# The own term of the second mixer as a row sum: one change to an encoder trunk kernel on one Trainium2 core

## The chip, the cores and the metric

The kernel runs on one core of a Trainium2 chip. The core has five engines that run side by side, each through its own list of instructions in order: TensorE (PE, matrix products into the PSUM memory; its weight loads are listed apart as PEld), VectorE (DVE), ScalarE (ACT), GpSimd (POOL, which cannot read PSUM) and SyncE (SP, which here only issues DMAs). They wait for each other through semaphores. The metric is the device time of one execution in microseconds, median over runs.

## The reference

A trunk of two layers over 256 tokens of width 2048, float32. Each layer adds a token mixer and a gated feed-forward block with a depthwise convolution, each behind an RMSNorm; a last RMSNorm closes it. The first mixer is a bidirectional mLSTM with 8 heads. The second one, which the change touches, is a bidirectional gated linear recurrence (HGRN2) with 16 heads of 128 keys and 128 values. For one direction of a head:

```python
def _hgrn_chunk(s_st, xs):
    q, k, lf, v = xs
    L = q.shape[2]
    b = jnp.cumsum(lf, axis=2)
    lower = jnp.tril(jnp.ones((L, L), dtype=bool))
    rel = jnp.where(lower[:, :, None], b[:, :, :, None, :] - b[:, :, None, :, :], -jnp.inf)
    attn = jnp.einsum('bhtsk,bhsk->bhts', jnp.exp(rel) * q[:, :, :, None, :], k)
    o = jnp.einsum('bhts,bhsv->bhtv', attn, v) + jnp.einsum('bhtk,bhkv->bhtv', q * jnp.exp(b), s_st)
...
    y = hgrn_direction(q, k_f, lf_f, v) + fl(hgrn_direction(fl(q), fl(k_b), fl(lf_b), fl(v)))
    y = y.reshape(b, s, B_V).astype(hn.dtype)
    y = head_rmsnorm(y, head_g, B_HEADS) * jax.nn.silu(g)
    return y @ w_out
```

A token is in the sum of both directions, and for s = t the decay is exp(0) = 1. So token t contributes to its own output v[t] times the sum over the keys of q[t] * (k_f[t] + k_b[t]). This is the own term.

## The kernel before

**Projections.** Tokens lie along the free axis and features on the 128 partitions. The weights stream from HBM in pieces (`split_weights`): a DMA brings 128x2048 float32, ScalarE rounds a half of it to `wh` (L145) and VectorE forms the rest `wl` (L146). `stream` then walks a list of chunks. A "fm" chunk gives two blocks of 128 features over 256 tokens; for each of its 16 slices of the depth PE does a product of 512 columns (L196) and one of 256 (L197) per block. A "tm" chunk gives 512 features with tokens on the partitions, three products of 512 columns (L186 to L188) per slice and token half. When a chunk is done its function `done` takes the result out of PSUM.

**Side work.** The work of a mixer's heads is written as Python generators that yield a delay. `Side.tick` is called between the products of the stream and resumes each generator whose delay has passed. So the small products of a head stand between the large ones of the projections in PE's list. The program is then put in order by a scheduler that works with its own estimate of times, and this order is fixed in the built program: on the chip each engine takes its list as it stands, and PE cannot go past a small product whose operands are late.

**A head of the second mixer.** Four heads form a quad; per quad there are six fm chunks (q and the two gates of each head), a tm chunk for V after the third and one for the output gate at the end. `take` turns a chunk's block into z, the gates g (ScalarE's sigmoid, VectorE's L586), the keys `KZ` of both directions, and on GpSimd the products q*g (`QZ`, L587), a copy of g (L589) and `ks`, the sum of the two keys (L592). With the second gate the generator `head` is pushed.

`head` builds the 256x256 matrix `AT` of weights between tokens. It starts with the own term: PE multiplies ks by q for each half of the tokens (L616; the whole 128x128 block, of which only the diagonal is wanted), and VectorE's `put` copies it into AT under the mask `ident` (L604, a copy under a predicate). Then a step passes (`yield step`, 2.4 in the scheduler's units, 1.9 for the last two heads). Then come seven levels of blocks of 1, 2, 4, ... 64 tokens. In each level PE multiplies the gathered keys `km` by the gathered queries `qm` (L626), VectorE multiplies KZ and QZ by the gates of that level (L627, L628) and gathers for the next level (L609), GpSimd multiplies the gates pairwise (L633), and `put` copies the level's part into AT under its mask. Last come the two blocks off the diagonal (L638 to L640), the product of AT with V into `py` (L651), a copy of it to `y` by ScalarE (L652) and the sums of squares (L655). `finish` normalises y and multiplies it by the gate (L666), transposes it (L672) and stores it for the output projection.

**GpSimd and VectorE beside each other.** Per head GpSimd does about ten instructions, nearly all of them in one burst when the second gate is there. The norm of each layer (L253) holds another product with a column of ones: the squares as the stationary operand, `ones[:, 0:1]` as the moving one.

Of the kernel before, what the change touches and what calls it, by code (L numbers as in the profile page):

```python
# [8 lines left out]
F32 = mybir.dt.float32  # L9
# [3 lines left out]
ALU = mybir.AluOpType  # L13
PSUM = bass.MemoryType.PSUM

P = 128
T = 256
# [35 lines left out]
def trunk_kernel(ctx, tc, xT, pp_d, cst_d, w_first, w_aq, w_ak, w_av, w_ao, w_aout,  # L53
                 w_bq, w_bv, w_bg, w_bout, w_up, w_down, out, mscr, stop=9):
    nc = tc.nc
    act, dve, pool, pe = nc.scalar, nc.vector, nc.gpsimd, nc.tensor
# [9 lines left out]
    ones = keep.tile([P, T], F32, name="ones")  # L66
# [4 lines left out]
    ident = cst[:, C_ID:C_ID + P]  # L71
# [5 lines left out]
    def aux(name):  # L77
        return psa.tile([P, 512], F32, tag="aux", name=name)
# [132 lines left out]
    def fm_scaled(ps, R, dst, scale=None):  # L211
        fm_sum(ps, dst)
        if scale is None:
            dve.tensor_tensor(dst, dst, R, ALU.mult)
        else:
            dve.scalar_tensor_tensor(dst, dst, scale, R, ALU.mult, ALU.mult)
# [75 lines left out]
    def head_scale(ss, width):  # L292
        rs = ev.tile([P, 2], F32, tag="rs", bufs=6, name="rs")
        dve.tensor_scalar(rs, ss, 1.0 / width, EPS, ALU.mult, ALU.add)
        pool.tensor_tensor(rs, rs, hmx, ALU.pow)
        return rs
# [238 lines left out]
    def hgrn(norm, nxt):  # L535
# [24 lines left out]
        def blocks(z, h, a, b):  # L560
            v = z[:, 0:2 * (T + h)].rearrange("k (p x) -> k p x", p=2)[:, :, a:b]
            return v.rearrange("k p (m j) -> k m p j", j=2 * h)[:, :, :, 0:h]

        def gview(g, n, start, h):
            v = g[:, start:start + 2 * (n - 1)].rearrange("k (p x) -> k p x", p=2)[:, :, 0::2]
            return v.rearrange("k p m -> k m p").unsqueeze(3).broadcast_to([P, n // 2, 2, h])

        def take(hd, what, ps):
            mp = box["mp"]
            st = heads[hd]  # L570
            if what == 0:
                st["q"] = mp.tile([P, T], F32, tag="q", bufs=2, name="q")
                fm_scaled(ps, norm.R, st["q"], box["oml"][:, hd:hd + 1])
                st["QK"] = mp.tile([P, 1152], F32, tag="QK", bufs=2, name="QK")
                st["G"] = mp.tile([P, 768], F32, tag="G0", bufs=2, name="G")
                return
            dr = what - 1
            lb, oml = box["lb"], box["oml"]
            QZ, KZ, G = st["QK"][:, 0:512], st["QK"][:, 512:1024], st["G"]
            z = mp.tile([P, T], F32, tag="z", bufs=2, name="z")  # L580
            fm_scaled(ps, norm.R, z)
            g = G[:, dr * T:(dr + 1) * T]
            kz = KZ[:, dr * T:(dr + 1) * T]
            act.activation(g, z, AF.Sigmoid)
            act.activation(kz, z, AF.Sigmoid, scale=-1.0)
            dve.tensor_scalar(g, g, oml[:, hd:hd + 1], lb[:, hd:hd + 1], ALU.mult, ALU.add)  # L586
            pool.tensor_tensor(QZ[:, (1 - dr) * T:(2 - dr) * T], st["q"], g, ALU.mult)  # L587
            if dr == 0:
                pool.tensor_copy(G[:, 512:768], g)  # L589
            else:  # L590
                st["ks"] = mp.tile([P, T], F32, tag="ks", bufs=2, name="ks")
                pool.tensor_tensor(st["ks"], KZ[:, 0:T], KZ[:, T:2 * T], ALU.add)  # L592
                side.push(head(hd))

        def head(hd):
            mp = box["mp"]
            st = heads[hd]
            QZ, KZ = st["QK"][:, 0:640], st["QK"][:, 512:1152]
            q, ks, G = st["q"], st["ks"], st["G"]
            AT = mp.tile([P, 4, P], F32, tag="AT", bufs=2, name="AT")  # L600
            pool.memset(AT[:, 0::3], 0.0)

            def put(ps, mask):
                dve.copy_predicated(AT[:, 0::3], mask.bitcast(I32).unsqueeze(1).broadcast_to([P, 2, P]),  # L604
                                    ps[:, 0:T].rearrange("p (a b) -> p a b", a=2))

            def gather(z, h, tag):
                m = mp.tile([P, T], F32, tag=tag, bufs=MIX, name=tag)
                dve.tensor_copy(m.rearrange("k (m p j) -> k m p j", p=2, j=h), blocks(z, h, 0, T))  # L609
                return m  # L610

            km, qm = gather(KZ, 1, "km"), gather(QZ, 1, "qm")
            pd = aux("pd")
            for t in range(2):
                c = slice(t * P, (t + 1) * P)
                pe.matmul(pd[:, c], ks[:, c], q[:, c], start=True, stop=True)  # L616
            put(pd, ident)
            step = SPREAD if hd < BH - 2 else STEP
            yield step
            n = T  # L620
            for li, h in enumerate(LEVELS):
                pd = aux("pd")
                qa, ka = blocks(QZ, h, 0, T), blocks(KZ, h, 0, T)
                for t in range(2):
                    c = slice(t * P, (t + 1) * P)
                    pe.matmul(pd[:, c], km[:, c], qm[:, c], start=True, stop=True)  # L626
                dve.tensor_tensor(ka, ka, gview(G, n, 1, h), ALU.mult)  # L627
                dve.tensor_tensor(qa, qa, gview(G, n, n + 1, h), ALU.mult)  # L628
                if h < 64:
                    km, qm = gather(KZ, 2 * h, "km"), gather(QZ, 2 * h, "qm")  # L630
                    n //= 2
                    G2 = mp.tile([P, 3 * n], F32, tag=f"G{h}", bufs=2, name="G2")
                    pool.tensor_tensor(G2, G[:, 0:6 * n:2], G[:, 1:6 * n:2], ALU.mult)  # L633
                    G = G2
                put(pd, cst[:, C_LV + li * P:C_LV + (li + 1) * P])
                yield step
            pd = aux("pd")
            pe.matmul(pd[:, 0:P], KZ[:, 0:P], QZ[:, T + P:2 * T], start=True, stop=True)  # L638
            pe.matmul(pd[:, P:T], KZ[:, T + P:2 * T], QZ[:, 0:P], start=True, stop=True)
            act.copy(AT[:, 1:3], pd[:, 0:T].rearrange("p (a b) -> p a b", a=2))  # L640
            yield
            while "V" not in st["qd"]:
                yield
            V, j = st["qd"]["V"], hd % 4
            py = aux("py")
            y = mp.tile([P, T], F32, tag="y", bufs=4, name="y")
            ss = mp.tile([P, 2], F32, tag="ss", bufs=2, name="ss")
            for t in range(2):
                c = slice(t * P, (t + 1) * P)
                for s in range(2):  # L650
                    pe.matmul(py[:, c], AT[:, 2 * s + t], V[:, s, j * P:(j + 1) * P], start=(s == 0), stop=(s == 1))  # L651
            act.copy(y, py[:, 0:T])  # L652
            for t in range(2):
                jk = ev.tile([P, T], F32, tag="jk", bufs=1, name="jk")
                act.activation(jk[:, 0:P], y[:, t * P:(t + 1) * P], AF.Square, accum_out=ss[:, t:t + 1])  # L655
            st["y"] = (y, head_scale(ss, 128))
# [109 lines left out]
    if stop > 1:  # L766
        c, close0 = ffn(0, n1, n2)
        chunks += c
    if stop > 2:
        c = hgrn(n2, n3)  # L770
# [7 lines left out]
    if stop > 3:  # L778
        c, close1 = ffn(1, n3, nf)
# [93 lines left out]
```

## Time and profile before

| | |
|---|---|
| median of 3 runs | 2469.77 us (2469.3 to 2469.8) |
| the profiled execution: its time | 2469.78 us |
| the profiled execution: its span | 2468.0 us |
| mean clock granted to PE | 0.998 |
| second mixer's heads | about 1146 to 1650 us of the span |

The profile is one execution recorded by the hardware. Its page lists the busy time of each engine, a picture of the span in slices, the chain of work that ended last (followed back from the last instruction to whatever released it), and the costliest groups of instructions with line, engine, operation, operands and shapes, count, busy time, mean duration in ns, and the idle time of the engine ahead of them with what ended it. Further views of the same trace give busy times in stretches of the span, and single instructions in order of time. There a row shows start and duration in us, engine, line and operands; instructions of the same group that follow each other share a row. A float32 product appears as two records. Durations of products overlap on PE, so the step from one start to the next is the price of a product in the stream, not its duration. The line of a helper (such as L604 in `put`) gathers all uses of the helper.

### The profile page before, as it was taken

Reading aid. Unit: us, or ns where it says so; the run is one execution under the profiler, and the core shown is the slowest. Engines: PE = TensorE matmul, PEld = TensorE weight load, DVE = VectorE, ACT = ScalarE, POOL = GpSimd, SP = SyncE. Lnnn points to the kernel's source line nnn. Section 1 sums busy time; section 2 is a strip of 40 time slices with the busy share of each in tenths; the row PEclk is TensorE's granted clock in tenths of the full one; section 3 lists DMA queues with packets and bytes.
Section 4 is the critical chain, followed back from the end, with each engine's and each line's share of the span. In section 5 each row is a group of like instructions: output and inputs, shape, how many; then the busy total and the mean of one; then the engine's idle time right before and its main releaser. Section 6 shows DMA issues by size and latency. Waiting matters only on the chain.

```text
span 2468.0 us, 35972 instructions
## 1 busy us (share of the span) xinstructions
PE 2450.2 (99%) x13950; PEld 2134.1 (86%) x13950; DVE 1781.9 (72%) x2975; ACT 1200.8 (49%) x1810; POOL 272.8 (11%) x341
## 2 busy tenths in 40 slices
PE   9999999999999999999999999999999999999998
PEld 7888888888888888888888888888888888888887
DVE  7766577777656777678888888887777755677754
ACT  6655455444444445444444444445544444444443
POOL 0100032000000000132222222224000000000022
PEclk9999999999999999999999999999999999999999
DMA  7654555666556555555454544446555555666553
GB/s 260 189 178 167 177 183 188 190 189 191 186 189 199 188 188 189 180 194 178 157 168 154 164 161 156 163 145 202 187 189 188 188 188 190 192 192 193 183 190 124
DMA packets 65915, 449.07 MB, mean 182 GB/s; under 512 B 7616, under 2 KB 8128, under 8 KB 15568
## 3 DMA queue, kind: packets, MB, share of 16 engines
q1 hardware_dynamic: 63936, 443.29, 55.4%
q0 software_dynamic: 800, 2.16, 0.6%
q8 instruction: 109, 1.79, 0.3%
q10 hardware_dynamic: 1008, 1.32, 0.1%
q14 instruction: 62, 0.51, 0.1%
HBM read 444.58 MB, written 2.16 MB: 181 GB/s over the span
## 4 chain that ended last, share of the span: by engine, by line
PE 90%; DVE 7%; issue 1%; ACT 1%; DMA 0%; DVEq 0%; POOL 0%; POOLq 0%
PE mm L196 50%; PE mm L197 25%; PE mm L187 3%; PE mm L188 3%; PE mm L186 3%; DVE wl L146 3%; DVE QK L627 1%; PE pd L626 1%; DVE km L609 1%; PE pn L439 1%; PE mm L175 1%; DVE AT L604 1%; PE py L651 1%; DVE qm L609 1%; DVE G L586 0%
## 5 line engine op out<-in xcount | busy, mean ns | idle before, releaser
L146 DVE TENSOR_TENSOR wl<-raw,wh 128x1024 fp32r<-128x1024 f32 (+1 forms) x864 | 1047.1, 1213 | 553.6 <-ACT wh L145 540.6
L145 ACT CAST wh<-raw 128x1024 fp32r<-128x1024 f32 (+1 forms) x864 | 884.4, 1024 | 895.8 <-PE mm L196 500.4
L196 PE MATMUL mm<-xt,wh 128*128 128x512 f32 x3776 | 1318.5, 395 | 0.0
L197 PE MATMUL mm<-xt,wl 128*128 128x256 f32 x3776 | 1050.8, 278 | 0.0
L196 PEld LDWEIGHTS mm<-xt,wh 128*128 128x128 f32 x3776 | 708.0, 188 | 161.2
L197 PEld LDWEIGHTS mm<-xt,wl 128*128 128x128 f32 x3776 | 709.9, 188 | 0.9
L196 PE MATMUL mm<-g,wh 128*128 128x512 f32 x1334 | 462.6, 394 | 0.0
L197 PE MATMUL mm<-g,wl 128*128 128x256 f32 x1334 | 369.5, 277 | 0.0
L196 PEld LDWEIGHTS mm<-g,wh 128*128 128x128 f32 x1334 | 250.1, 188 | 58.1
L197 PEld LDWEIGHTS mm<-g,wl 128*128 128x128 f32 x1334 | 250.4, 188 | 0.0
L186 PE MATMUL mm<-wh,xt 128*128 128x512 f32 x512 | 203.9, 402 | 2.2 <-ACT xt L203 2.2
L187 PE MATMUL mm<-wl,xt 128*128 128x512 f32 x512 | 204.5, 399 | 0.4 <-DVE wl L146 0.4
L188 PE MATMUL mm<-wh,xt 128*128 128x512 f32 x512 | 201.9, 396 | 0.0
L208 ACT COPY b<-mm 128x256 f32<-128x256 f32 x237 | 87.7, 370 | 178.9 <-PE mm L197 178.9
L242 POOL TENSOR_TENSOR acc<-hx 128x256 f32<-128x256 f32 x4 | 4.8, 1205 | 1239.7 <-DVE hx L311 1239.7
L186 PEld LDWEIGHTS mm<-wh,xt 128*128 128x128 f32 x512 | 96.1, 189 | 21.0 <-ACT xt L203 2.5
L187 PEld LDWEIGHTS mm<-wl,xt 128*128 128x128 f32 x512 | 97.0, 189 | 18.4 <-DVE wl L146 0.8
L188 PEld LDWEIGHTS mm<-wh,xt 128*128 128x128 f32 x512 | 97.0, 189 | 18.4
L196 PE MATMUL mm<-yb,wh 128*128 128x512 f32 x256 | 89.6, 396 | 0.0
L196 PE MATMUL mm<-ya,wh 128*128 128x512 f32 x256 | 89.1, 394 | 0.0
L245 POOL TENSOR_TENSOR sq<-hx 128x256 f32<-128x256 f32 x52 | 62.1, 1202 | 197.8 <-DVE hx L311 195.6
L209 DVE TENSOR_TENSOR a<-mm,b 128x256 f32<-128x256 f32 x86 | 36.5, 424 | 51.0 <-ACT b L208 50.9
(185 smaller groups left out, 2083.2 us busy)
## 6 DMA issues: line engine op xcount, KB each, us to landing
raw<-in_w_up SPq DMA_DIRECT2D x172, 1024.0 KB, 5.2
raw<-in_w_down SPq DMA_DIRECT2D x64, 1024.0 KB, 4.9
raw<-in_w_bq SPq DMA_DIRECT2D x48, 1024.0 KB, 5.1
raw<-in_w_ao SPq DMA_DIRECT2D x16, 1024.0 KB, 4.9
raw<-in_w_aout SPq DMA_DIRECT2D x16, 1024.0 KB, 5.2
raw<-in_w_bv SPq DMA_DIRECT2D x16, 1024.0 KB, 4.9
raw<-in_w_bg SPq DMA_DIRECT2D x16, 1024.0 KB, 4.9
raw<-in_w_bout SPq DMA_DIRECT2D x16, 1024.0 KB, 5.1
```

Source lines behind the costliest of these rows:

```text
L145: act.copy(wh[:, :m], r)
L146: dve.tensor_tensor(wl[:, :m], r, wh[:, :m].bitcast(F32), ALU.subtract)
L175: pe.matmul(ps[f][:, 0:T], w[:, c:c + P], x[:, o:o + T], start=(k + kk == 0 and i == 0), stop=(k + kk == ch.nk - 1 and i == 2))
L186: pe.matmul(ps[t], xh, wh[:, c], start=st, stop=False)
L187: pe.matmul(ps[t], xh, wl[:, c], start=False, stop=False)
L188: pe.matmul(ps[t], xl, wh[:, c], start=False, stop=sp)
L196: pe.matmul(ps[f], wh[:, c:c + P], x, start=st, stop=False)
L197: pe.matmul(ps[f][:, 0:T], wl[:, c:c + P], x[:, 0:T], start=False, stop=sp)
L208: act.copy(b, ps[:, T:2 * T])
L209: dve.tensor_tensor(dst, ps[:, 0:T], b, ALU.add)
L245: eng.tensor_tensor(s, hT[k], hT[k], ALU.mult)
L609: dve.tensor_copy(m.rearrange("k (m p j) -> k m p j", p=2, j=h), blocks(z, h, 0, T))
```

## The change

The own term is no longer a part of AT. GpSimd multiplies ks by q right after summing the keys. PE sums this product over the keys by a product with one column of ones for each half of the tokens, and ScalarE copies the two columns out as `own`. At the end VectorE takes y from PSUM as V * own + py, in place of ScalarE's copy. The masked copy with `ident` and the step behind the own term go.

```diff
                 st["ks"] = mp.tile([P, T], F32, tag="ks", bufs=2, name="ks")
                 pool.tensor_tensor(st["ks"], KZ[:, 0:T], KZ[:, T:2 * T], ALU.add)
+                pool.tensor_tensor(st["ks"], st["ks"], st["q"], ALU.mult)
                 side.push(head(hd))
...
             km, qm = gather(KZ, 1, "km"), gather(QZ, 1, "qm")
             pd = aux("pd")
+            own = mp.tile([P, 2], F32, tag="own", bufs=2, name="own")
             for t in range(2):
-                c = slice(t * P, (t + 1) * P)
-                pe.matmul(pd[:, c], ks[:, c], q[:, c], start=True, stop=True)
-            put(pd, ident)
+                pe.matmul(pd[:, t:t + 1], ks[:, t * P:(t + 1) * P], ones[:, 0:1], start=True, stop=True)
+            act.copy(own, pd[:, 0:2])
             step = SPREAD if hd < BH - 2 else STEP
-            yield step
             n = T
...
-            act.copy(y, py[:, 0:T])
+            for t in range(2):
+                c = slice(t * P, (t + 1) * P)
+                dve.scalar_tensor_tensor(y[:, c], V[:, t, j * P:(j + 1) * P], own[:, t:t + 1], py[:, c],
+                                         ALU.mult, ALU.add)
```

In the changed kernel the lines behind the first added one move by one to three: the multiplication on GpSimd is L593, the own product L617, and the copy of `own` L618; the level products stay at L626.

More of the change, by code (lines that the diff above doesn't have):

```diff
@@ L598, in head @@
             QZ, KZ = st["QK"][:, 0:640], st["QK"][:, 512:1152]
-            q, ks, G = st["q"], st["ks"], st["G"]
+            ks, G = st["ks"], st["G"]
             AT = mp.tile([P, 4, P], F32, tag="AT", bufs=2, name="AT")
```

## The prediction

> **What bounds the kernel now.** I read the page first: busy times, then the chain of work that ended last.
>
> ```profile
> span 2468.0 us, 35972 instructions
> PE 2450.2 (99%) x13950; PEld 2134.1 (86%) x13950; DVE 1781.9 (72%) x2975; ACT 1200.8 (49%) x1810; POOL 272.8 (11%) x341
> PE 90%; DVE 7%; issue 1%; ACT 1%; DMA 0%; DVEq 0%; POOL 0%; POOLq 0%
> ```
>
> PE is busy for 99% of the span and carries 90% of the chain. Every microsecond taken off PE, or waited by it, goes into the time. The 7% that the chain spends on VectorE must lie somewhere, so next I read busy times by stretch. The second mixer's heads run from about 1146 to 1650 us, in eight pairs of heads some 66 us apart; one pair begins at about 1207. The columns are the stretch, its length, then busy time (and instructions) of PE, PEld, DVE, ACT and POOL, then clock and DMA.
>
> ```profile
> 1146.00:1650.00 504.00, 501.27 (x2881) 436.03 (x2880) 441.40 (x907) 226.41 (x375) 129.54 (x187) 1.00 0.49 157
> 1207.00:1254.00 47.00, 46.79 (x268) 40.43 (x267) 46.78 (x105) 20.57 (x33) 14.28 (x20) 1.00 0.44 143
> 1254.00:1273.00 19.00, 19.00 (x117) 16.77 (x116) 12.65 (x21) 10.11 (x19) 2.09 (x4) 1.00 0.58 185
> ```
>
> PE is idle for only 2.7 of 504 us. But the second row shows that VectorE is full too: 46.78 of 47.00 us. Only in the last 19 us of a pair has it 6.35 us to spare. So the stage has two bounds at once. PE sets the time, and VectorE, which prepares the operands of the mixer's small products (gathers L609, multiplications L627 and L628), must not fall behind, since PE takes its instructions in order and a small product that is not ready stops the projections behind it.
>
> **The change part by part.** *The own product on PE.* The question is what a product with a single column costs.
>
> ```profile
> L616 PE MATMUL pd<-q,ks 128*128 128x128 f32 x64 | 9.7, 274 | 0.0
> L253 PE MATMUL pc<-ones,acc 128*128 128x1 f32 x16 | 2.0, 229 | 0.0
> 1212.97 0.28 PE L197 MATMUL mm<-xt,wl 128*128 128x256 f32 x1
> 1213.09 0.60 PE L616 MATMUL pd<-q,ks 128*128 128x128 f32 x4
> 1213.45 0.47 PE L196 MATMUL mm<-xt,wh 128*128 128x512 f32 x1
> 1213.76 0.27 PE L197 MATMUL mm<-xt,wl 128*128 128x256 f32 x1
> 410.23 0.27 PE L197 MATMUL mm<-xt,wl 128*128 128x256 f32 x1
> 410.34 0.50 PE L253 MATMUL pc<-ones,acc 128*128 128x1 f32 x4
> 410.70 0.47 PE L196 MATMUL mm<-xt,wh 128*128 128x512 f32 x1
> 411.02 0.28 PE L197 MATMUL mm<-xt,wl 128*128 128x256 f32 x1
> ```
>
> The norms hold the very form that the change puts in (L253: float32 squares stationary, one column of ones moving). Both kinds appear as four records for two products. Read starts, not durations, because products overlap. From the L197 ahead to the L197 behind it is 1213.76 - 1212.97 = 0.79 us with four records of 128 columns, and 411.02 - 410.23 = 0.79 us with four records of one column. The price does not follow the columns. Sixteen heads times the difference, 0.00 (0.01 is what the rows resolve), is 0.0 us, at most 0.2 either way. PE gains nothing.
>
> *ScalarE and the queues.* No DMA is added or moved. Sixteen copies of y from PSUM (256 columns) go, sixteen copies of 2 columns come. It is busy 226.41 of 504 us, and the weight conversions queued behind the new copy are made ahead of need, so I cost it at nothing; VectorE's and PE's work covers it.
>
> *VectorE, its own work.* Per head one masked copy goes (L604 of the own term) and two instructions y = V * own + py come, 128x128 each, for which the nearest row is L666.
>
> ```profile
> L604 DVE COPY_PREDICATED AT<-cst,pd 128x256 f32<-128x256 int32 x128 | 55.5, 436 | 0.7
> L666 DVE SCALAR_TENSOR_TENSOR y<-y,rs,sg 128x128 f32<-128x128 f32 x32 | 9.3, 341 | 0.2 <-POOL rs L295 0.2
> 1216.66 0.44 DVE L604 COPY_PREDICATED AT<-cst,pd 128x256 f32<-128x256 int32 x1
> 1216.99 0.41 DVE L628 TENSOR_TENSOR QK<-QK,G 128x256 f32<-128x256 f32 x1
> ```
>
> Over the stage that is 32 x 0.341 - 16 x 0.436 = 10.9 - 7.0 = +3.9 us. The place matters more: the masked copies leave the full stretch (0.33 us each from start to start, 0.67 a pair), while in the built order the new instructions stand behind all gathers of their pair, close to where VectorE has its 6.35 us to spare. They are covered there.
>
> *The order on PE.* The own term was a step of its own in the head's generator; with `yield step` gone every level product is issued one step (2.4) earlier. The order of the built programs shows what this does. Between a pair's first own product and the second level product of that head stood 8 projection products of 512 columns and 7 of 256; now 5 and 5. Up to the fourth level product of the pair's second head stood 91 and 14; now 83 and 12. The numbers of small products ahead are the same. So PE comes to these two places earlier by 3 x 0.23 + 2 x 0.12 = 0.92 us and by 8 x 0.23 + 2 x 0.12 = 2.08 us, while VectorE's list up to the operand is longer by one gather (about 0.2 us) at the first place and shorter by two masked copies (0.67 us) at the second. What slack was there?
>
> ```profile
> 1231.80 0.39 PE L188 MATMUL mm<-wh,xt 128*128 128x512 f32 x1
> 1232.03 0.40 PE L186 MATMUL mm<-wh,xt 128*128 128x512 f32 x1
> 1232.17 0.56 DVE L609 COPY qm<-QK 128x256 f32<-128x256 f32 x2
> 1232.63 1.13 PE L626 MATMUL pd<-qm,km 128*128 128x128 f32 x8 [0.21 <-DVE qm L609]
> 1215.11 0.29 DVE L609 COPY qm<-QK 128x256 f32<-128x256 f32 x1
> 1216.64 0.61 PE L626 MATMUL pd<-qm,km 128*128 128x128 f32 x4
> 1240.60 0.28 DVE L609 COPY qm<-QK 128x256 f32<-128x256 f32 x1
> 1241.95 0.61 PE L626 MATMUL pd<-qm,km 128*128 128x128 f32 x4
> ```
>
> The first four rows show the price of a 512-column product (0.23, start to start) and the one place in a pair where PE waits today: the product follows 0.60 behind L186 instead of 0.23, because gathers that start at 1232.17 come late. That is about 0.4 us a pair; the last of the two gathers ends at 1232.73 and the first about 0.14 before PE starts, which I take as the least handover. At the first place the gather is ready at 1215.40 and used at 1216.64: 1.24 us of slack become 1.24 - 0.92 - 0.20 = 0.12, just none left. At the second it is 1241.95 - 1240.88 = 1.07, and becomes 1.07 - 2.08 + 0.67 = -0.34: with the handover a new wait of 0.48 us a pair, beside the old one. This is term A. It is 0 if VectorE meets fewer delays than today, which I take as its low end.
>
> *GpSimd.* Sixteen multiplications of 128x256 come.
>
> ```profile
> L592 POOL TENSOR_TENSOR ks<-QK 128x256 f32<-128x256 f32 x16 | 14.8, 924 | 66.6 <-ACT QK L585 66.6
> L587 POOL TENSOR_TENSOR QK<-q,G 128x256 f32<-128x256 f32 x32 | 27.0, 843 | 134.2 <-DVE G L586 134.2
> L216 DVE SCALAR_TENSOR_TENSOR q<-q,oml,R 128x256 f32<-128x256 f32 x16 | 11.7, 728 | 0.2
> L216 DVE SCALAR_TENSOR_TENSOR q<-q,R 128x256 f32<-128x256 f32 x8 | 3.4, 420 | 0.2
> 1209.01 0.89 POOL L592 TENSOR_TENSOR ks<-QK 128x256 f32<-128x256 f32 x1 [6.61 <-ACT QK L585]
> 1210.13 0.78 POOL L587 TENSOR_TENSOR QK<-q,G 128x256 f32<-128x256 f32 x1 [0.23 <-DVE G L586]
> 1210.21 0.97 DVE L216 SCALAR_TENSOR_TENSOR q<-q,oml,R 128x256 f32<-128x256 f32 x1
> 1210.87 4.39 POOL L633 TENSOR_TENSOR G<-G 128x384 f32<-128x384 f32 x6
> 1211.11 1.26 DVE L627 TENSOR_TENSOR QK<-QK,G 128x256 f32<-128x256 f32 x1
> ```
>
> At 0.84 to 0.92 us each they are 13.5 to 14.8 us of GpSimd, which is busy 129.54 of 504; that is no bound by itself. The own product does not wait either: the sum ends at 1209.90, the multiplication would end near 1210.9, and PE reads it at 1213.09. But the new instruction stands inside a burst. In the first head of a pair it is queued ahead of L587 and the six L633, so these, and VectorE's gather and multiplications that read them, come up to 0.9 us later. And VectorE is slow while GpSimd runs: the same kind of instruction (L216) takes 728 ns in this mixer and 420 in the first one, where GpSimd has no such work beside it; here one took 0.97 next to L587, and L627 took 1.26, against the 0.41 of L628 above. One such neighbour costs VectorE 0.55 (0.97 - 0.42) to 0.85 us (1.26 - 0.41). This is term B, twice a pair. Low end 0, where VectorE would be reading PSUM meanwhile or finish first; high end 0.9, the whole instruction; I take 0.6, near the lower row, since the second head's multiplication stands behind the first L633 and meets more conversions. The stretch is full, so nothing makes up for it before the place of term A: what VectorE loses PE waits.
>
> The Trainium skill, SBUF — State Buffer, section "Who interferes with whom", says that GpSimd and VectorE share one pair of SBUF ports under an exclusive lock, and that a VectorE instruction with two SBUF inputs blocks fully while a GpSimd instruction that reads SBUF holds it. The rows above agree in direction; by that rule term B would be the whole 0.9, and the sum below 2487.5.
>
> *Sum.* Seven pairs with 0.48 + 2 x 0.6 = 1.68 us, and the first pair, whose own product the built order puts 3 us later, with term B alone, 1.2: 13.0 us. On the profiled execution's own 2469.78 us (span 2468.0 and 1.8 around it; the median of the runs is 2469.77, the same) this gives 2482.8 us. With both terms at their low ends it is 2469.8; with B at 0.9 it is 7 x 2.28 + 1.8 = 17.8, so 2487.5.
>
> **The rivals.** *The waits are absorbed.* VectorE loses two masked copies in the full stretch (0.67 us a pair, 5.3 in all) and so gains more than it loses, if GpSimd's extra work falls beside instructions that read PSUM. For it: PE's whole idle time in the stage is 2.7 us today. Against it: the slack at the second place falls by 1.4 us whatever GpSimd does. It gives 2469.8, or 2467.1 if the 2.7 go too; not slower. It decides where term B is under 0.1 us and A is nought.
>
> *A product of one column is cheap.* If, in this stage, four records of one column cost no more than one projection product of 256 columns (0.12) instead of 0.79 - 0.12 - 0.23 = 0.44, PE would save 16 x 0.32 = 5.1 us: 2464.7 if nothing else happened. Against it stands the L253 group, in the same form and between the same neighbours.
> The Trainium skill, TensorE: Matmul & The Clock Gate, section "Back-to-back issue gap", gives an isolated floor of about 25 ns for up to 64 columns, by which (estimate) 64 records would save some 5.5 us; the same section says that weight loads count too, and the trace sides with that.
>
> *PE waits for GpSimd itself.* If the multiplication came more than 2.2 us later than worked out (1213.09 - 1210.9), PE would stop at the own product of every head. Only a queue full of L633 ahead of it could do this; in the built order at most one stands ahead. One further microsecond would cost 16 us beside the 13: 2499.
>
> **How the numbers follow.** Forecast 0.70, absorbed waits 0.20, cheap product 0.05, PE waiting for GpSimd 0.05. What a measurement of this kernel can tell from no change is about 0.2%, 4.9 us. Of the forecast's 0.70 about 0.04 stays under that bound (A at nought with B at 0.3), and of the absorbed waits none gets below it. Faster 0.05, same 0.24, slower 0.71. The range reaches from 2470, into the absorbed case, to 2490, just over the upper bound of B; the forecast's own range is 2474 to 2489.
>
> **What would show it.** In the profile after: own products with one column must again stand 0.79 us from L197 to L197. PE's idle time in the stage should rise from 2.7 to some 10 to 16 us, named as VectorE's gather qm, at the second to fourth level products. VectorE's full stretch should stay full, with the mean of gathers and L627 longer than today. If PE's idle time stays under 4 us, terms A and B are wrong; if PE waits for GpSimd at the own product, the third rival is right.

## The result and the profile after

The changed kernel takes 2478.99 us (median of 6 runs, 2478.57 to 2479.6) where the kernel before takes 2469.59 (6 runs, 2469.16 to 2469.89): a ratio of 1.0037, 95% interval 1.0027 to 1.0047, 9.4 us slower. The profiled execution has a span of 2477.3 us, 9.3 more than before.

First the page of the kernel after: span, busy times, and the shares of the chain of work that ended last.

```profile
span 2477.3 us, 36047 instructions
PE 2452.0 (99%) x13950; PEld 2133.6 (86%) x13950; DVE 1795.6 (72%) x2991; ACT 1195.8 (48%) x1810; POOL 283.1 (11%) x357
PE 89%; DVE 8%; issue 2%; ACT 1%; DMA 0%; DVEq 0%; SPq 0%; POOL 0%; POOLq 0%
```

PE has the same number of records as before (x13950) and still carries the chain. VectorE's busy time grew by 13.7 us, GpSimd's by 10.3.

Where do the 9.3 us lie? The surest measure is how many product records PE gets done in a fixed stretch. The next two fences are busy times of PE by stretch (stretch, length, busy time and records, clock, DMA share, GB/s), before and then after: the heads' stage, and 70 us of the output projection behind it.

```profile
1146.00:1650.00 504.00, 501.27 (x2881) 1.00 0.49 157
1670.00:1740.00 70.00, 70.00 (x405) 1.00 0.61 195
```

```profile
1146.00:1650.00 504.00, 495.63 (x2836) 1.00 0.48 155
1670.00:1740.00 70.00, 70.00 (x398) 1.00 0.58 183
```

In the stage 45 records fewer were done. A record there is worth 504 / 2881 = 0.175 us, so the stage costs 7.9 us more. Behind it 7 of 405 are missing, at 0.173 us each: 1.2 us, with PE busy throughout and the clock at 1.00. Together 9.1 of the 9.3. The second piece is no part of the change's work; it comes back below as a pace of PE. A count of records takes in waits and pace alike, so in the stage too a few records can be pace. There PE is idle for 504 - 495.63 = 8.4 us, 5.6 more than before.

The view of waits names the cause in the stage: engine, tile and line that waited, and for whom, then total us, times, longest. Before:

```profile
PE pd L626 <- DVE qm L609: 2.7, 8, 1.4
```

After:

```profile
PE pd L626 <- DVE qm L610: 7.7, 12, 1.0
```

In the stage PE waits for one thing only, VectorE's gather of the queries, and not for GpSimd, ScalarE or a DMA. The view names 5.0 us more. A listed wait is less than it costs, since the records overlap. In the second pair of heads, in order of time on PE (start, duration):

```profile
1234.23 0.39 PE L188 MATMUL mm<-wh,xt 128*128 128x512 f32 x1
1234.46 0.50 PE L617 MATMUL pd<-ones,ks 128*128 128x1 f32 x4
1234.99 1.13 PE L626 MATMUL pd<-qm,km 128*128 128x128 f32 x8
1236.86 0.68 PE L626 MATMUL pd<-qm,km 128*128 128x128 f32 x4 [0.74 <-DVE qm L610]
1237.29 0.48 PE L186 MATMUL mm<-wh,xt 128*128 128x512 f32 x1
```

Eight records at 0.11 us are 0.89; PE took 1236.86 - 1234.99 = 1.87 to the next one, so this wait cost 0.98, not 0.74. With such 0.24 on each of twelve waits, and 0.16 on each of the eight before (0.37 by the starts in the rows of the prediction, 0.21 listed), the 5.0 us become an estimated 6.6 of the 7.9; what makes up the rest is not shown (a product that is late by less than the overlap leaves no idle time and is not listed, and some of it may be pace). The rows also show the place: the second head's own product and three level products stand together, with no projection product between them. By the built order these three are the second head's first level, the first head's sixth, and the second head's second level, which waits. The third of the stack waits by as much (0.72 to 0.74 listed) in all six pairs from the second to the seventh. On VectorE and GpSimd at the same time:

```profile
1230.84 0.93 POOL L633 TENSOR_TENSOR G<-G 128x384 f32<-128x384 f32 x1
1231.00 1.05 DVE L628 TENSOR_TENSOR QK<-QK,G 128x256 f32<-128x256 f32 x1
1231.73 0.92 POOL L593 TENSOR_TENSOR ks<-ks,q 128x256 f32<-128x256 f32 x1
1231.97 1.18 DVE L627 TENSOR_TENSOR QK<-QK,G 128x256 f32<-128x256 f32 x1
1232.98 1.48 DVE L146 TENSOR_TENSOR wl<-raw,wh 128x1024 fp32r<-128x1024 f32 x1
1235.77 0.73 DVE L627 TENSOR_TENSOR QK<-QK,G 128x256 f32<-128x256 f32 x2
1236.43 0.48 DVE L610 COPY qm<-QK 128x256 f32<-128x256 f32 x2
```

L627 took 1.18 us beside the new multiplication L593, where two of them together took 0.73 at 1235.77. The last gathers run from 1236.43 to 1236.91, and with the first of the two PE goes on at 1236.86.

One listed wait follows the multiplication itself. It stands at the second level of the very first head; first the changed kernel, then the changed kernel without the multiplication (run 4 below):

```profile
1151.75 0.71 PE L626 MATMUL pd<-qm,km 128*128 128x128 f32 x4 [0.68 <-DVE qm L610]
```

```profile
1151.00 0.71 PE L625 MATMUL pd<-qm,km 128*128 128x128 f32 x4
```

The seven versions that have the multiplication on GpSimd ahead of the levels (after and runs 1, 3, 7, 8, 10, 12) all wait here, 0.44 to 0.69 us. Without it there (before and runs 2, 4, 6, 9, 11) nothing waits, and with it on VectorE (run 5) it is 0.07.

### The profile page after: what moved, and what is told of

Same layout as the page of the kernel before. It is cut to its first block, busy times and chain, and to the rows that moved or that the text cites. A ratio compares the mean times of both kernels' runs of the same rounds, so it can differ in the third digit from the quotient of the medians.

```text
span 2477.3 us, 36047 instructions
## 1 busy us (share of the span) xinstructions
PE 2452.0 (99%) x13950; PEld 2133.6 (86%) x13950; DVE 1795.6 (72%) x2991; ACT 1195.8 (48%) x1810; POOL 283.1 (11%) x357
## 4 chain that ended last, share of the span: by engine, by line
PE 89%; DVE 8%; issue 2%; ACT 1%; DMA 0%; DVEq 0%; SPq 0%; POOL 0%; POOLq 0%
PE mm L196 50%; PE mm L197 25%; PE mm L187 3%; PE mm L188 3%; PE mm L186 3%; DVE wl L146 3%; DVE QK L627 2%; PE pd L626 1%; DVE km L610 1%; DVE QK L628 1%; DVE qm L610 1%; PE pn L439 1%; PE mm L175 1%; PE py L651 1%; DVE AT L605 1%
## 5 line engine op out<-in xcount | busy, mean ns | idle before, releaser
L146 DVE TENSOR_TENSOR wl<-raw,wh 128x1024 fp32r<-128x1024 f32 (+1 forms) x864 | 1049.3, 1215 | 548.6 <-ACT wh L145 532.8
L626 PEld LDWEIGHTS pd<-qm,km 128*128 128x128 f32 x448 | 62.7, 190 | 18.0 <-PE pd L626 6.3
```

The costliest lines, as they stand in the source:

```text
L146: dve.tensor_tensor(wl[:, :m], r, wh[:, :m].bitcast(F32), ALU.subtract)
```

## The experiments

One table first. Each run is compared with the kernel before on the same chip (medians 2469.4 to 2469.7). "Stage" and "pace" are the records done from 1146 to 1650 and from 1670 to 1740 us, as above, and "accounts for" is the records missing against 2881 and 405 at 0.175 and 0.173 us each. "Waits" is PE's listed wait in the stage.

| run | time | ratio, 95% interval | stage | waits | pace | accounts for |
|---|---|---|---|---|---|---|
| before | 2469.6 | | 2881 | 2.7 | 405 | |
| after | 2479.0 | 1.0037 [1.0027, 1.0047] | 2836 | 7.7 | 398 | 9.1 |
| 1 step back | 2472.2 | 1.0010 [1.0001, 1.0019] | 2874 | 4.6 | 399 | 2.3 |
| 2 before, no step | 2471.7 | 1.0009 [1.0000, 1.0017] | 2876 | 2.5 | 398 | 2.1 |
| 3 before, multiplication | 2492.4 | 1.0093 [1.0080, 1.0107] | 2835 | 10.1 | 399 | 9.1, rest below |
| 4 no multiplication | 2472.6 | 1.0013 [1.0004, 1.0022] | 2870 | 3.4 | 399 | 3.0 |
| 5 multiplication on VectorE | 2472.8 | 1.0014 [1.0005, 1.0023] | 2868 | 3.2 | 399 | 3.3 |
| 6 own product late | 2486.8 | 1.0070 [1.0058, 1.0083] | 2867 | 3.7 | 399 | 3.5, rest below |
| 7 distance 2.8 | 2470.9 | 1.0006 [0.9997, 1.0015] | 2882 | 3.1 | 398 | 1.0 |
| 8 two multiplications | 2481.2 | 1.0048 [1.0035, 1.0061] | 2827 | 9.1 | 399 | 10.5 |
| 9 before, distance 2.8 | 2469.4 | 1.0000 [0.9991, 1.0009] | 2894 | 1.6 | 397 | -0.9 |
| 10 two records, 2.8 | 2474.5 | 1.0020 [1.0011, 1.0029] | 2826 | 8.1 | 399 | see there |
| 11 late, more products | 2473.0 | 1.0014 [1.0006, 1.0023] | 2875 | 3.5 | 399 | 2.1 |
| 12 two records, 3.4 | 2471.3 | 1.0009 [1.0000, 1.0019] | 2850 | 5.4 | 398 | see there |

Any edit makes the scheduler arrange the small products anew. Only run 8 has the lists of PE and VectorE of the changed kernel unaltered; all others change the order as well as the work, and each row is one profiled execution.

### 1. The step put back

```diff
             step = SPREAD if hd < BH - 2 else STEP
+            yield step
             n = T
```

> The changed kernel with the step behind the own term put back, everything else as changed. If the lost step (PE coming to the small products earlier, term A) is the cause of the 9.4 us, the time falls to 2470 to 2473 us and PE's idle time in the stage falls back to about 3 us. If the added GpSimd multiplication (term B) is the cause, it stays at 2476 to 2480 us. If both count, about the middle, 2473 to 2476.

Measured: 2472.18, 6.8 us below the changed kernel and in the range of the lost step. With the step back the multiplication on GpSimd and the missing masked copies together cost 2.5 us, of which 1.2 is the stage.

### 2. The kernel before without the step

```diff
             step = SPREAD if hd < BH - 2 else STEP
-            yield step
             n = T
```

> The kernel before with only the step behind the own term taken out; the own term is still a 128x128 product and a masked copy. Term A alone: 2474 to 2478 us if the lost step is the cause, 2469 to 2471 if the GpSimd multiplication is. The two masked copies a pair are still on VectorE here, so if anything the wait is larger than term A by up to 0.67 us a pair (5 us).

Measured: 2471.66, 2.0 us over before, 0.9 of it in the stage, where the stretch is now:

```profile
1146.00:1650.00 504.00, 501.36 (x2876) 1.00 0.48 157
```

The waits are 2.5 us, no more than before, and PE is idle for 2.64 us where it was 2.73. So the five records that are missing are not waits but pace: the lost step by itself makes PE wait no longer.

### 3. The kernel before with an unread multiplication

```diff
                 pool.tensor_tensor(st["ks"], KZ[:, 0:T], KZ[:, T:2 * T], ALU.add)
+                kq = mp.tile([P, T], F32, tag="kq", bufs=1, name="kq")
+                pool.tensor_tensor(kq, st["ks"], st["q"], ALU.mult)
```

> The kernel before with one more GpSimd multiplication per head (sum of the keys times q into a tile that nothing reads). Term B alone: 2474 to 2479 us if GpSimd's neighbour slows VectorE by 0.6 us twice a pair, 2469 to 2471 us if the lost step is the cause.

Measured: 2492.43, more than the whole change. The waits of PE in the stage, and then two stretches of this run (columns as above):

```profile
PE pd L628 <- DVE qm L611: 10.1, 9, 1.9
```

```profile
1146.00:1650.00 504.00, 493.86 (x2835) 1.00 0.48 155
...
1850.00:2350.00 500.00, 500.00 (x2831) 1.00 0.57 186
```

The stage lost 46 records, 8.0 us, or 0.50 us for each of the sixteen multiplications: with the masked copies in place and the step kept, and in the order that came out, one costs PE about half its length on average. The waits stand where they stood before, at the second level of a pair's second head. In the second pair that wait was 0.21; now it is:

```profile
1233.98 1.13 PE L628 MATMUL pd<-qm,km 128*128 128x128 f32 x8 [1.04 <-DVE qm L611]
```

The other 14 us lie where the heads have long ended: from 1850 to 2350 us PE is never idle and does 55 records fewer than the kernel before, whose row for this stretch is:

```profile
1850.00:2350.00 500.00, 500.00 (x2886) 1.00 0.59 189
```

Run 6 shows the same, and run 11 what it is not.

### 4. The changed kernel without the multiplication

```diff
                 pool.tensor_tensor(st["ks"], KZ[:, 0:T], KZ[:, T:2 * T], ALU.add)
-                pool.tensor_tensor(st["ks"], st["ks"], st["q"], ALU.mult)
```

This leaves out the factor q in the own term.

> The changed kernel without the GpSimd multiplication; left out is the factor q in the own term, so the column sums the two keys alone. If term B is the cause, the time falls to 2469 to 2472 us; if the lost step is, it stays at 2475 us or more. If the cause is neither but the new VectorE instructions at the end of a head, e1 to e3 move little and this one stays at 2478 to 2480.

Measured: 2472.56, 6.4 us below the changed kernel. Either part taken back, the step (run 1) or the multiplication, removes some two thirds of the loss; 6.8 + 6.4 is more than the 9.4 there is. The two terms are not additive. The stage row of this run:

```profile
1146.00:1650.00 504.00, 500.54 (x2870) 1.00 0.48 157
```

Of its 1.9 us of missing records only 0.7 is idle time of PE (3.46 for 2.73).

### 5. The multiplication on VectorE

```diff
-                pool.tensor_tensor(st["ks"], st["ks"], st["q"], ALU.mult)
+                dve.tensor_tensor(st["ks"], st["ks"], st["q"], ALU.mult)
```

> The changed kernel with the extra multiplication on VectorE instead of GpSimd; nothing else differs. Known so far: without that multiplication the changed kernel takes 2472.6, with it 2479.0. Theory 'neighbour' (the multiplication costs because GpSimd reads and writes beside VectorE's copies, which then take longer): on VectorE the same work costs only its own 0.3 to 0.4 us a head, 5 to 6 us of VectorE's time in all, part of it in its idle time before the burst of a pair: 2473 to 2476, and VectorE's copies in the stage are as short as without the multiplication. Theory 'burst' (VectorE has no time left in the first half of a pair, whoever adds to it): the own work lands in the full stretch and the time is 2478 to 2481.

Measured: 2472.83, just under the range of "neighbour" (2473 to 2476). In the stage, group of this line on VectorE (count, busy time, mean ns, idle):

```profile
L593 DVE TENSOR_TENSOR ks<-ks,q 128x256 f32<-128x256 f32 x15 | 13.7, 913 | 0.0
```

The expectation said 0.3 to 0.4 us each; it took 0.91. PE waited 3.2 us, 4.5 less than with the work on GpSimd, so "burst" falls. VectorE did not become busier by the 13.7 us: over the span it is busy for 1791.3 us, where the changed kernel has 1795.6 and run 4, without the multiplication, 1786.3. Its other instructions were shorter by more than half of what was added; the gather of the keys, for one, took 305 ns on average in the stage, and 333 in run 4. That speaks for "neighbour", but the order changed too. In this order there are 0.9 us of projection products between the second head's own product and the level products behind it, not none.

### 6. Own product and multiplication behind the level loop

```diff
-                pool.tensor_tensor(st["ks"], st["ks"], st["q"], ALU.mult)
...
-            pd = aux("pd")
-            own = mp.tile([P, 2], F32, tag="own", bufs=2, name="own")
-            for t in range(2):
-                pe.matmul(pd[:, t:t + 1], ks[:, t * P:(t + 1) * P], ones[:, 0:1], start=True, stop=True)
-            act.copy(own, pd[:, 0:2])
             step = SPREAD if hd < BH - 2 else STEP
+            yield step
...
             act.copy(AT[:, 1:3], pd[:, 0:T].rearrange("p (a b) -> p a b", a=2))
+            kq = mp.tile([P, T], F32, tag="km", bufs=MIX, name="kq")
+            pool.tensor_tensor(kq, ks, st["q"], ALU.mult)
+            pd = aux("pd")
+            own = mp.tile([P, 2], F32, tag="own", bufs=2, name="own")
+            for t in range(2):
+                pe.matmul(pd[:, t:t + 1], kq[:, t * P:(t + 1) * P], ones[:, 0:1], start=True, stop=True)
+            act.copy(own, pd[:, 0:2])
```

> The changed kernel with its loop step put back, and with the multiplication, the one-column product and the small copy moved behind the level loop of the head, so that GpSimd multiplies after the burst in which VectorE is behind. Theory 'neighbour and place' (the cost is the multiplication standing beside VectorE's burst, together with own product and three level products put close to one another): nothing of it is left, the masked copies are gone, and the time is 2466 to 2470, waits of PE for VectorE's gather in the stage at or below those of the kernel before. Theory 'the multiplication costs wherever it stands' (0.4 us a head): 2473 to 2477. A third outcome, 2470 to 2473, is what putting back the step alone gave (2472.2): the place of the multiplication would then be worth nothing.

Measured: 2486.77, a clear miss. The stage is not to blame (2867 records, waits 3.7 us). One stretch behind it:

```profile
1850.00:2350.00 500.00, 500.00 (x2832) 1.00 0.57 185
```

Against the kernel before, 54 of 2886 records are missing, 1.9%; over the 725 us from 1740 to the end that is 13.6 us. Without it the run would stand near 2473, the third outcome: the place of the multiplication is worth nothing against run 1.

### 7. The planned distance of level products, 2.8 for 2.4

```diff
-SPREAD = 2.4
+SPREAD = 2.8
```

> The changed kernel with the planned distance of a head's level products set from 2.4 to 2.8 us of TensorE's list, so that the second head's own product and its first level products do not stand as close to one another. If the 9.4 us come from level products that stand closer than VectorE can gather for them, about half of the 1.1 us at the second head's start and the 0.36 us behind it goes: 2471 to 2475. If the cost is VectorE's lost time alone and does not depend on the order, nothing changes: 2478 to 2480. A planner that now fits fewer steps beside the projections could also push the heads' ends past the stage: over 2482.

Measured: 2470.85, ratio 1.0006 [0.9997, 1.0015]: against before no difference that these runs can tell, and 0.15 below the range expected. Every instruction of the changed kernel is in it; only the order differs, and 8.1 us are gone. PE, VectorE and GpSimd around the same place of the same pair:

```profile
1231.38 0.78 POOL L593 TENSOR_TENSOR ks<-ks,q 128x256 f32<-128x256 f32 x1
...
1234.25 0.50 PE L617 MATMUL pd<-ones,ks 128*128 128x1 f32 x4
1234.61 1.82 PE L626 MATMUL pd<-qm,km 128*128 128x128 f32 x12
...
1235.32 0.48 DVE L610 COPY qm<-QK 128x256 f32<-128x256 f32 x2
...
1236.19 0.47 PE L188 MATMUL mm<-wh,xt 128*128 128x512 f32 x1
```

The stack of own product and three level products is there too, at the same time (1234.25 against 1234.46), with the multiplication at nearly the same place. One difference is what VectorE has behind it: in this order four, not five, level products of the first head stand ahead of the stack. So the gathers that the third of the stack needs start at 1235.32 instead of 1236.43, 1.11 us earlier, and PE goes through. The same goes for all six pairs whose third of the stack waited 0.72 to 0.74: none of these waits is left. Of the four that are listed still, three are in the first pair and one in the last.

### 8. A second, unread multiplication

```diff
                 pool.tensor_tensor(st["ks"], st["ks"], st["q"], ALU.mult)
+                kq = mp.tile([P, T], F32, tag="kq", bufs=1, name="kq")
+                pool.tensor_tensor(kq, KZ[:, 0:T], st["q"], ALU.mult)
```

> The changed kernel with a second multiplication of the same size on GpSimd behind the first, whose result nothing reads; TensorE's and VectorE's lists around a pair are those of the changed kernel. If the slack of the pair is used up (the cost of a multiplication then falls in full on TensorE, 6.4 us for the first one), the second adds as much or more: 2484 to 2488, with TensorE's waits for VectorE's gathers in the stage longer by 5 to 8 us. If the first one cost only because of the wait that it made at one place, the second is free: 2479 to 2481. If the run is far above 2488 and the heads' stage is not longer by as much, the rest is TensorE's slower pace after the stage, as with the unread multiplication put into the kernel before.

Measured: 2481.20, 2.2 us over the changed kernel: far from the 5 to 9 of the first branch, and 0.2 above the range of "free". Its rows on GpSimd tell why:

```profile
1224.75 1.18 POOL L595 TENSOR_TENSOR kq<-QK,q 128x256 f32<-128x256 f32 x1 [8.00 <-ACT QK L585]
...
1231.70 0.92 POOL L593 TENSOR_TENSOR ks<-ks,q 128x256 f32<-128x256 f32 x1
```

It reads only operands that are ready early, and the scheduler put it ahead, into time in which GpSimd had been idle for 8 us. There the sixteen cost 2.2 / 16 = 0.14 us each. Of the same kind of instruction, one in GpSimd's burst cost 0.50 (run 3). What a multiplication costs depends on where it stands; this run is not a dose at the same place, so it does not test the "slack used up" branch as meant.

### 9. The kernel before with distance 2.8

```diff
-SPREAD = 2.4
+SPREAD = 2.8
```

> The kernel before with the planned distance of level products 2.8 instead of 2.4: the control for the run in which this distance took the changed kernel from 2479.0 to 2470.9. If the wider distance repairs what the lost step does to the order, it gives the kernel before little: 2468 to 2471. If it is simply the better setting for any version, worth some 8 us, the kernel before falls to 2461 to 2464. If it is too wide once the step is there as well (a head then takes 2.8 more), the pair ends late: 2473 or more.

Measured: 2469.44, ratio 1.0000. The distance is not a better setting for any version: in the stage it gives 13 records (2.3 us), and the slower pace behind it takes 1.4 back.

### 10. and 12. The own product in two records

```diff
-SPREAD = 2.4
+SPREAD = 2.8
...
-                st["ks"] = mp.tile([P, T], F32, tag="ks", bufs=2, name="ks")
+                st["ks"] = mp.tile([P, T], F32R, tag="ks", bufs=2, name="ks")
...
-                pe.matmul(pd[:, t:t + 1], ks[:, t * P:(t + 1) * P], ones[:, 0:1], start=True, stop=True)
-            act.copy(own, pd[:, 0:2])
+                pe.matmul(pd[:, 2 * t:2 * t + 2], ks[:, t * P:(t + 1) * P], onesr, start=True, stop=True)
+            act.copy(own, pd[:, 0:4])
```

Run 12 differs from run 10 by a distance of 3.4.

> The changed kernel with distance 2.8 and with the own product in the one-pass number type of the large products (its stationary operand rounded to it, two columns of ones, so two records a head instead of four). If a record of such a small product costs 0.11 us whatever its columns, a head saves 0.22 us and the kernel 3.6 us against the run with distance 2.8 alone (2470.9): 2466 to 2468.5, below the kernel before. If the price hangs on something else (the change of type, the columns), nothing is saved: 2470 to 2472. If the order that the scheduler makes of it falls badly, waits of PE in the stage rise again and it is over 2474.

> The run with the two-record own product again (2474.5 at distance 2.8, where TensorE waited 8.1 us for gathers), now with distance 3.4: in the built order only three level products, not four, of a pair's first head stand ahead of the second head's own product, and the level products behind it are further apart. If the order sets the waits, they fall below 3 us and, with 3.6 us of records saved, the run comes to 2464 to 2468, below the kernel before. If the waits belong to the changed type or to VectorE's lost time, they stay at 8 us: 2473 to 2476. A wide distance may also let the last heads end late (waits at the transposes or the output projection behind 1650 us), and TensorE's slower pace, should it set in, adds up to 13 us with no wait; both would be seen in their own stretch.

Run 10 measured 2474.46, run 12 2471.31, both above before. The price of a record came out as expected. The first rows are PE in the changed kernel, with four records of one column; the second those of run 10, with two records of two:

```profile
1214.59 0.39 PE L196 MATMUL mm<-xt,wh 128*128 128x512 f32 x1
1214.82 0.50 PE L617 MATMUL pd<-ones,ks 128*128 128x1 f32 x4
1215.19 0.36 PE L197 MATMUL mm<-xt,wl 128*128 128x256 f32 x1
1215.39 0.40 PE L196 MATMUL mm<-xt,wh 128*128 128x512 f32 x1
```

```profile
1214.01 0.39 PE L197 MATMUL mm<-xt,wh 128*128 128x512 f32 x1
1214.23 0.28 PE L619 MATMUL pd<-onesr,ks 128*128 128x2 f32 x2
1214.37 0.37 PE L198 MATMUL mm<-xt,wl 128*128 128x256 f32 x1
1214.58 0.40 PE L197 MATMUL mm<-xt,wh 128*128 128x512 f32 x1
```

From one 512-column product to the next it is 0.80 with four records and 0.57 with two; without a small product it is 0.23 + 0.12 = 0.35. So four cost 0.45 and two 0.22. The number type and the columns changed with the records, so that it is the records is read from the equal 0.11 each in all three forms. Over sixteen heads that saves 3.6 us, but the new order gave it away again: waits of 8.1 us at distance 2.8 (the third outcome of run 10) and 5.4 at 3.4, where under 3 were expected; run 12's time lies between its two ranges. By records, 2826 and 2850 plus the 32 saved are 23 fewer than before and one more, so run 12 only paid the waits with the saving. The wider distance was not the lever that run 7 had made it seem. It helped there because of the order that came out.

### 11. Run 6 with more small products at the norms

```diff
                     pe.matmul(self.pc[t][:, 0:1], s[:, t * P:(t + 1) * P], ones[:, 0:1],
                               start=(k == KT - 3 or not self.final), stop=(k == KT - 1))
+                if not self.final:
+                    pe.matmul(self.pc[0][:, 1:2], s[:, 0:P], ones[:, 0:1], start=True, stop=True)
```

> The run with the own product moved behind the loop (2486.8), with one more unread one-column product at each of the row sums of the norms (two records, 0.22 us each, under 1 us in all). There TensorE kept a pace of 353 ns for a pair of projection products from 1675 us to the end, 13 us above the pace of 347 ns, without a wait. If that pace is a state that a few small products can switch, this run falls back to 2472 to 2476, or switches at another place. If it belongs to what stands in the stage before (the data, the place of operands in memory), it stays at 2486 to 2489.

Measured: 2472.97, 13.8 us below run 6 although PE has more to do. The norm behind the output projection now has six records instead of four (this run, PE in order of time):

```profile
1749.98 0.50 PE L253 MATMUL pc<-ones,acc 128*128 128x1 f32 x4
1750.35 0.36 PE L256 MATMUL pc<-ones,acc 128*128 128x1 f32 x2
```

Here are 70 us ahead of that norm and 70 behind it, in this run and then in run 6, whose norm is at the same place:

```profile
1679.90:1749.90 70.00, 70.00 (x398) 1.00 0.57 184
1754.00:1824.00 70.00, 70.00 (x407) 1.00 0.58 187
```

```profile
1679.90:1749.90 70.00, 70.00 (x398) 1.00 0.58 184
1754.00:1824.00 70.00, 70.00 (x399) 1.00 0.57 181
```

Ahead of it both are slow. Behind it this run does 407 records and run 6 still 399. So the pace went back at this norm here and not in run 6. That two more records are the reason is not shown: the changed kernel has four at its norm (at 1756.82) and goes back as well.

```profile
1679.90:1749.90 70.00, 70.00 (x398) 1.00 0.57 183
1760.00:1830.00 70.00, 70.00 (x407) 1.00 0.58 185
```

So do runs 1, 2, 4, 5, 7 to 10 and 12 with four records; only runs 3 and 6 stay slow. Runs 6 and 11 also differ a little in the order of the small products in the stage. But the extra 14 us of run 6 are not the price of the moved multiplication, which run 11 has as well; that those of run 3 are the same pace follows from the equal count (2831 and 2832), not from a run of its own.

## Why the prediction came out: right in kind, by terms that do not add

*The own product on PE: right.* Four records of one column cost 0.45 us, as against 0.79 - 0.35 = 0.44 before; PE gained nothing. The rival of a cheap product falls: the price goes with the records, 0.11 each (run 10).

*ScalarE and VectorE's own work: right.* No wait of PE names ScalarE in the stage. The new instructions for y take what was forecast (341 ns), and VectorE is idle for 4.7 us ahead of them. In the stage:

```profile
L654 DVE SCALAR_TENSOR_TENSOR y<-V,own,py 128x128 f32<-128x128 f32 x28 | 8.4, 343 | 4.7 <-PE py L651 4.7
```

*Term A, the order: a mechanism that shows only with the multiplication there, wrong in its place, and too large.* The forecast put a new wait at the fourth level product of the second head. It came earlier, at that head's second level product, the third of a stack that the lost step had closed up; at the first head's second level nothing waited from the second pair on, as worked out (in the first pair it did, by the multiplication). Alone, the order adds no wait with the masked copies in place (run 2) and 0.7 us of idle PE with them gone (run 4; 1.9 by records), against 7 x 0.48 = 3.4.

*Term B, the neighbour: right in size as what VectorE loses.* By the pages VectorE is busy for 1795.6 us in the changed kernel and 1786.3 without the multiplication (run 4): 9.3 us, 0.58 for each, against the 0.6 taken. In run 3 it is 1793.3 against 1781.9 before: 11.4 us, 0.71 each. Of that PE lost 8.0 us, 0.50 each. One sign did not come as said: in the stage the mean of L627 fell from 544 to 531 ns and that of the gather of the keys from 377 to 351; the gather of the queries (310 to 337), L628 (448 to 498) and the conversion L146 (1250 to 1275) became longer. The Trainium skill, SBUF — State Buffer, section "Who interferes with whom", has a VectorE instruction with two SBUF inputs block fully while GpSimd reads SBUF. In the rows after, L627 starts at 1231.97 and L593 ends at 1231.73 + 0.92 = 1232.65. Blocked to there (0.68) and then its usual 0.41 would be 1.09; it took 1.18, so the trace agrees for that instruction, roughly. The sum by that rule, 2487.5, was too high: over all multiplications the runs show a loss of VectorE of 0.45 (run 1) to 0.71 (run 3), not 0.9.

*The sum: the step that failed.* It took all that VectorE loses for a wait of PE ("what VectorE loses PE waits") and added A on top. In run 1 VectorE is busy for 1793.5 us, 7.2 more than in run 4, where the changed kernel has 9.3 more; but the stage lost only 1.2 us. With the masked copies gone and the step kept, most of B was absorbed. It lost 1.9 with the order alone (run 4) and 7.9 with both. That the missing masked copies make room for one of the two and not for both (5.3 us of VectorE, the argument of the rival "the waits are absorbed") fits these numbers and is not shown by a run of its own. That rival fell for this kernel but describes the same instructions in another order (run 7). Of the forecast's 13.0 the stage shows 7.9; that the total of 9.4 comes nearer is partly luck, since 1.2 of it is the pace, which no part of the forecast had.

*The rival that PE waits for GpSimd itself: it fell.* The view of waits has no such row.

How much of the 7.9 us belongs to the multiplication and how much to the lost step stays open: taking either away also rearranges the lists, and no run here removed the work and kept the order.

None of the versions is faster than the kernel before.

## What to carry to other kernels

Where one engine's list is full and another takes small products from it in a fixed order, two small disturbances that are each nearly absorbed can be dear together (1.2 and 1.9 us of the stage here, and 7.9 with both), so work out slack for the whole list with all edits in, not edit by edit. Before an edit is blamed for its work, run the same instructions in another order (a distance, a step): here that alone moved 8.1 of 9.4 us. An extra instruction on GpSimd was cheap in its idle time (0.14 us each) and dear in the burst (0.50), so look where the scheduler puts it.

## What the runs showed of the hardware

PE has two paces in the same stream of projection products, with nothing waiting and the clock at 1.00. In 500 us it did 2886 records in the kernel before and 2831 and 2832 in runs 3 and 6, 1.9% fewer, which is some 14 us by the end. Between 1670 and 1740 us the kernel before alone has the full pace (405 records); all thirteen others have 397 to 399. The pace holds over hundreds of microseconds. At the norm behind the output projection, a group of four small products (six in run 11), it went back to the full one in eleven versions and not in runs 3 and 6. Why is open; before the first norm behind the mixer alone it makes 1.2 of the change's 9.4 us.

The price of a small product followed its records (0.45 us for four, 0.22 for two), with one or 128 columns in float32 and with two in the one-pass type.
